# Mean over the last axis: an exit in which four engines only report, and GpSimd clears early and awaits the last store

## The chip, the cores and the metric

One core of a Trainium2 chip. The metric is the device time of one execution in microseconds (us). In the ten profiles it is 1.4 to 1.9 us longer than the span, because the span runs from the first to the last instruction of the kernel, and the measured time also holds part of what the runtime does around it.

## The reference

```python
def setup_inputs():
    return {"x": np.random.randn(64, 256, 8192).astype(np.float32)}

def reference(x):
    return np.mean(x, axis=2)
```

537 MB are read, and 16,384 means are written.

## The kernel before

The rows are loaded in 8 MB pieces into three buffers by SyncE's DMA queue. VectorE sums them, ScalarE helps at the end. The last 4 MB come in shrinking chunks so that little is left to sum after the last byte, and the final 512 bytes are stored by SyncE:

```python
    untracked(scaled_sum(fin[1][:, 0:1], fin_in[:, 0 : lastw + k]))._wait_ge(sem, 16)
    with tc.issue_after(st.ins):
        last_store = store_last(1)      # transpose on VectorE, DMA issued by SyncE
```

The exit is rewritten by hand after the program is built. A barrier of two semaphores stands there: each engine *reports* by a DRAIN that adds 1 to a gather semaphore (number 96), GpSimd *gathers* (waits for 4, takes 4 off), and *releases* the others by adding 4 to a second semaphore (97), on which each of them waits and takes 1 off. In between GpSimd *clears* the kernel's own semaphores (99 to 116) for the next execution. In the kernel before, the gather also waits for the last store:

```python
    drain, gather, release, _, clear = [
        i for i in exit_ins if i.engine == mybir.EngineType.Pool
    ][:5]
    ...
        for w in waits:
            if w.id != stored:
                nc.sync.wait_ge(bass.SemaphoreHandle(w.ant_name, w.id), w.wait_value)
    bass.BassInstruction(gather)._wait_ge(
        bass.SemaphoreHandle(last_store.ins.sync_info.on_update[0].ant_name, stored), 16
    )
    ...
    end_bb.instructions = [
        *awaits.instructions, *exit_ins[1 : exit_ins.index(drain)], drain, gather, clear, release
    ]
```

Of the kernel before, what the change touches and what calls it, by code (L numbers as in the profile page):

```python
# [18 lines left out]
def kernel(  # L19
# [5 lines left out]
    nc = tc.nc  # L25
# [26 lines left out]
    load_sem = [tc.alloc_semaphore(f"load{i}") for i in range(LOAD_SEMS)]  # L52
    tail_sem = [tc.alloc_semaphore(f"tail{i}") for i in range(len(LAST_CHUNKS) + 1)]
# [42 lines left out]
    def store_last(r):  # L96
        nc.vector.transpose(out=fin_t[r][:], in_=fin[r][:])  # L97
        return nc.sync.dma_start(out=out_last[r], in_=fin_t[r][0:P:SQ, :])
# [50 lines left out]
    with tc.issue_after(st.ins):  # L149
        last_store = store_last(1)  # L150
# [20 lines left out]
    blocks = nc.main_func.blocks  # L171
    end_bb, parent = blocks[2], nc.bb_map[body_bb.name]
# [3 lines left out]
    with nc.body("scratch", parent=parent, valid_engines=[DVE]):  # L176
        over = nc.vector.br_eq(nc.vector.zero_reg, 0, end_bb.name, "skipped").ins
    made = {b.name: b for b in blocks}
# [13 lines left out]
        name=nc.get_next_instruction_name(), engine=DVE, associate_branch=over.name  # L192
# [8 lines left out]



    exit_ins = list(end_bb.instructions)
    waiter, waits = exit_ins[0], exit_ins[0].sync_info.on_wait
    assert waiter.engine == mybir.EngineType.SP and isinstance(waiter, mybir.InstDrain)
    stored = last_store.ins.sync_info.on_update[0].id
    drain, gather, release, _, clear = [
        i for i in exit_ins if i.engine == mybir.EngineType.Pool
    ][:5]  # L210
    assert isinstance(clear, mybir.InstISA)
    with nc.body("awaits", parent=parent, valid_engines=[mybir.EngineType.SP]):
        for w in waits:
            if w.id != stored:
                nc.sync.wait_ge(bass.SemaphoreHandle(w.ant_name, w.id), w.wait_value)
    bass.BassInstruction(gather)._wait_ge(
        bass.SemaphoreHandle(last_store.ins.sync_info.on_update[0].ant_name, stored), 16
    )
    awaits = next(b for b in blocks if b.name == "awaits")
    blocks.remove(awaits)  # L220
    end_bb.instructions = [
        *awaits.instructions, *exit_ins[1 : exit_ins.index(drain)], drain, gather, clear, release
    ]


# [28 lines left out]
```

## Time and profile before

| | before |
|---|---|
| time, three runs | 1246.15 us (1246.12 to 1246.19) |
| span of the profiled run | 1244.4 us |
| DMA | 431 GB/s over the span |
| time of the profiled run (not one of the three) | 1246.25 us |
| last transpose ends | 1242.49 us |
| last store: issued, landed | 1242.515, 1244.063 us |
| last instruction ends | 1244.426 us |

The stream of loads sets all but the last 4 us. The change can only act after the last store has been issued, so that is where to read: the instructions of the exit, which do not count as busy time, and the trace's records of when each semaphore was counted. Two of those semaphores matter: that of the last store (116) and that of the runtime's own barrier behind the kernel (2), which is counted nine times per round. No view of the profile prints these counts; here and below they are read from the trace's records. A DMA has *landed* when its semaphore makes its last count. In the views, PEld is TensorE, ACT ScalarE, DVE VectorE, SP SyncE and POOL GpSimd; a q behind the name marks an instruction that does not count as busy.

### The profile page before, as it was taken

Reading aid. Unit: us, or ns where it says so; the run is one execution under the profiler, and the core shown is the slowest. Engines: PE = TensorE matmul, PEld = TensorE weight load, DVE = VectorE, ACT = ScalarE, POOL = GpSimd, SP = SyncE. Lnnn points to the kernel's source line nnn. Section 1 sums busy time; section 2 is a strip of 40 time slices with the busy share of each in tenths; the row PEclk is TensorE's granted clock in tenths of the full one; section 3 lists DMA queues with packets and bytes.
Section 4 is the critical chain, followed back from the end, with each engine's and each line's share of the span. In section 5 each row is a group of like instructions: output and inputs, shape, how many; then the busy total and the mean of one; then the engine's idle time right before and its main releaser. Section 6 shows DMA issues by size and latency. Waiting matters only on the chain.

```text
span 1244.4 us, 203 instructions
## 1 busy us (share of the span) xinstructions
DVE 1087.0 (87%) x78; ACT 16.5 (1%) x13; POOL 0.2 (0%) x4
## 2 busy tenths in 40 slices
DVE  2898988989889889898898988989889898898898
ACT  0000000000000000000000000000000000000004
POOL 0000000000000000000000000000000000000000
DMA  9999999999999999999999999999999999999998
GB/s 432 423 426 438 438 438 438 436 430 415 438 438 438 438 438 432 417 432 438 438 438 438 432 417 432 438 438 438 438 436 419 426 438 438 438 438 436 426 419 373
DMA packets 10241, 536.95 MB, mean 431 GB/s; under 512 B 1280, under 2 KB 1536, under 8 KB 1792
## 3 DMA queue, kind: packets, MB, share of 16 engines
q1 hardware_dynamic: 10240, 536.94, 99.8%
q14 instruction: 1, 0.01, 0.0%
HBM read 536.87 MB, written 0.07 MB: 431 GB/s over the span
## 4 chain that ended last, share of the span: by engine, by line
DMA 70%; DVE 29%; SPq 0%; issue 0%; DVEq 0%
DMA xt<-in_x_dram 70%; DVE res L80 29%; DVE fin_in L80 0%; SPq L70 0%; DVE fin_in L86 0%; DVE fin_t L97 0%; DVEq L86 0%
## 5 line engine op out<-in xcount | busy, mean ns | idle before, releaser
L80 DVE TENSOR_REDUCE res<-xt 128x2 f32<-128x16384 f32 (+1 forms) x63 | 1076.3, 17085 | 153.1 <-DMA xt<-in_x_dram 153.1
L83 ACT ACT_TABLE_LOAD x1 | 1.3, 1283 | 1181.0 <-DVE res L80 1181.0
L83 ACT ACTIVATE xt<-xt 128x8192 f32<-128x8192 f32 (+5 forms) x6 | 14.7, 2444 | 43.9 <-DMA xt<-in_x_dram 43.7
L80 DVE TENSOR_REDUCE fin_in<-xt 128x1 f32<-128x256 f32 (+3 forms) x5 | 5.0, 1005 | 0.3 <-DMA xt<-in_x_dram 0.2
L80 DVE TENSOR_REDUCE head<-xt 128x1 f32<-128x4096 f32 x1 | 4.4, 4420 | 0.7 <-DMA xt<-in_x_dram 0.7
L83 ACT ACTIVATION_READ_ACCUMULATOR xt<-xt 128x1 f32 x6 | 1.1, 186 | 0.0
L60 DVE MEMSET fin<- 128x32 f32 x2 | 0.1, 85 | 0.9 <-PEq L238 0.9
L86 DVE TENSOR_SCALAR_CACHE_REDUCE fin_in<-fin_in 128x265 f32<-128x265 f32 x1 | 0.4, 430 | 0.2 <-DVE fin_in L80 0.2
L97 DVE STREAM_TRANSPOSE fin_t<-fin 128x32 f32<-128x32 f32 x2 | 0.4, 212 | 0.1
L138 DVE TENSOR_SCALAR bulk<-res 128x126 f32<-128x126 f32 x1 | 0.2, 228 | 0.1
L86 DVE TENSOR_SCALAR_CACHE_REDUCE head<-head 128x2 f32<-128x2 f32 x1 | 0.2, 154 | 0.1
L238 POOL MEMSET const-bfloat16-1.0<- 128x1 bf16 x1 | 0.1, 102 | 0.0
L238 POOL MEMSET const-uint8-127<- 128x1 uint8 x1 | 0.1, 102 | 0.0
L238 POOL MEMSET const-float32-0.0<- 128x1 f32 x1 | 0.1, 99 | 0.2 <-issue 0.2
L238 POOL MEMSET const-float32-1.0<- 128x1 f32 x1 | 0.1, 99 | 0.0
L86 DVE DVE_READ_ACCUMULATOR fin_in<-fin_in 128x1 f32 x1 | 0.1, 83 | 0.0
L86 DVE DVE_READ_ACCUMULATOR head<-head 128x1 f32 x1 | 0.1, 82 | 0.0
## 6 DMA issues: line engine op xcount, KB each, us to landing
xt<-in_x_dram SPq DMA_DIRECT2D x1, 4096.0 KB, 31.2
xt<-in_x_dram SPq DMA_DIRECT2D x1, 2048.0 KB, 35.7
xt<-in_x_dram SPq DMA_DIRECT2D x1, 1024.0 KB, 37.7
xt<-in_x_dram SPq DMA_DIRECT2D x63, 40.8
xt<-in_x_dram SPq DMA_DIRECT2D x1, 512.0 KB, 38.5
xt<-in_x_dram SPq DMA_DIRECT2D x1, 256.0 KB, 38.7
xt<-in_x_dram SPq DMA_DIRECT2D x1, 128.0 KB, 38.6
fin_in<-in_x_dram SPq DMA_DIRECT2D x1, 128.0 KB, 38.5
```

Source lines behind the costliest of these rows:

```text
L60: nc.vector.memset(fin[r][:], 0.0)
L80: return untracked(nc.vector.tensor_reduce(out=dst, in_=src, axis=X, op=ADD))
L83: return untracked(nc.scalar.activation(out=src, in_=src, func=COPY, accum_out=dst))
L86: return nc.vector.tensor_scalar(out=src, in0=src, scalar1=inv, scalar2=None, op0=mybir.AluOpType.mult, op1=ADD, accum_out=dst,)
L97: nc.vector.transpose(out=fin_t[r][:], in_=fin[r][:])
L138: nc.vector.tensor_scalar_mul(out=bulk[:], in0=res[:], scalar1=inv)
L238: nc = _bacc.Bacc("TRN2", target_bir_lowering=False, num_devices=1)
```

## The change

The intent: engines that have reported need not be held, so the release goes; and the clear of the semaphores can run while the last store is still in flight, if that store's semaphore is left out and taken back to zero by the wait on it.

```diff
-    with nc.body("awaits", parent=parent, valid_engines=[mybir.EngineType.SP]):
-    ... (waits of SyncE, same in both)
...
-    bass.BassInstruction(gather)._wait_ge(
-        bass.SemaphoreHandle(last_store.ins.sync_info.on_update[0].ant_name, stored), 16
-    )
...
+    last_sem = bass.SemaphoreHandle(*sems[stored][:1], stored)
+    with nc.body("clears", parent=parent, valid_engines=[POOL]):
+        nc.gpsimd.sem_clear(range(used[0], stored))
+        nc.gpsimd.wait_ge(last_sem, 16).then_inc(last_sem, -16)
+    ...
+    reports = [
+        i
+        for i in exit_ins[1 : exit_ins.index(next(i for i in exit_ins if i.engine == POOL))]
+        if isinstance(i, mybir.InstDrain)
+    ]
+    drain, gather = [i for i in exit_ins if i.engine == POOL][:2]
     end_bb.instructions = [
-        *awaits.instructions, *exit_ins[1 : exit_ins.index(drain)], drain, gather, clear, release
+        *made["awaits"].instructions, *reports, drain, gather, *made["clears"].instructions
     ]
```

(`...` marks lines left out, here and in the cuts below.)

## The prediction

> **What bounds the kernel now.** I read the page first: the chain that ended last, then the same chain in order of time, then the views of single source lines for what stands after it. On the page:
>
> ```profile
> span 1244.4 us, 203 instructions
> DVE 1087.0 (87%) x78; ACT 16.5 (1%) x13; POOL 0.2 (0%) x4
> HBM read 536.87 MB, written 0.07 MB: 431 GB/s over the span
> DMA 70%; DVE 29%; SPq 0%; issue 0%; DVEq 0%
> ```
>
> The reader sees a kernel that streams 537 MB at one steady rate: the page's row of DMA tenths is 9 in all slices but the last, so the loads set the time. The 29% given to VectorE are reductions that free a buffer for a load already queued behind others. GpSimd (POOL) works for 0.2 us in all. The change touches nothing before the last load, so only the tail matters. The chain in order of time, from the last load on:
>
> ```profile
> 1201.66 38.49 DMA xt<-in_x_dram
> ...
> 1241.80 0.45 DVE fin_in L86 x2
> 1242.27 0.21 DVE fin_t L97
> ```
>
> The chain stops at 1242.48 with the transpose of the last results, but the span is 1244.4: some 1.9 us come after the last piece of arithmetic, in the store and the exit. These do not count as busy work, and the view of the lines that issue them shows them. First the last store's issue, the later of two, and the two waits of SyncE's exit (columns: engine and operation, count, shortest/median/longest ns, first and last start in us):
>
> ```profile
> L98 SPq DMA_DIRECT2D out_dram<-fin_t x2: 522/580/637, 1236.5 to 1242.5; - x2
> L215 SPq EVENT_SEMAPHORE  x2: 28/28/28, 1243.1 to 1243.2; - x2
> ```
>
> Then the exit itself, all under one line:
>
> ```profile
> L156 POOLq EVENT_SEMAPHORE  x2: 17/262/506, 1243.6 to 1244.3; - x2
> L156 POOLq DRAIN  x1: 41/41/41, 0.8 to 0.8; - x1
> L156 PEldq DRAIN  x1: 8/8/8, 0.9 to 0.9; - x1
> L156 ACTq DRAIN  x1: 536/536/536, 1240.9 to 1240.9; - x1
> L156 DVEq DRAIN  x1: 10/10/10, 1242.5 to 1242.5; - x1
> L156 SPq DRAIN  x1: 311/311/311, 1243.2 to 1243.2; - x1
> L156 POOLq EVENT_SEMAPHORE_RANGE_CLEAR  x1: 136/136/136, 1244.2 to 1244.2; - x1
> L156 SPq EVENT_SEMAPHORE  x1: 17/17/17, 1244.4 to 1244.4; - x1
> L156 PEldq EVENT_SEMAPHORE  x1: 51/51/51, 1244.4 to 1244.4; - x1
> ```
>
> To be seen here: four engines report by a DRAIN, SyncE last; GpSimd's first semaphore instruction (the gather) is the 506 ns one; the clear comes after it, then the 17 ns release, then each engine's wait on the release. The trace's records with their starts to the nanosecond, and its records of semaphore counts, give this ledger (us): store issued 1242.515, issue ends 1243.037; SyncE's DRAIN 1243.250 to 1243.561; gather 1243.586 to 1244.092; the last store's semaphore makes a first step at 1243.454 and its last at 1244.063; clear 1244.156 to 1244.292; release 1244.321 to 1244.338; TensorE's wait on it ends 1244.426, which is the end of the span. So **the store's landing at 1244.063 sets the exit**: the gather had SyncE's report at 1243.563 and sat 0.50 us for the store.
>
> **What the Trainium skill says.** (1) "DMA: Bandwidth & Descriptors", "Why a DMA increments its semaphore by 16 and not by 1": a transfer on fewer than 16 engines jumps by 16 less that number at once, and only the full 16 means landed. The trace agrees: the store writes four rows, and its semaphore shows one early step and then four, from 1244.005 to 1244.063. (2) The same page, "Anatomy of one DMA", puts most of about 2 us fixed cost into the receipt of the write. Here issue to landing is 1244.063 - 1242.515 = 1.55 us, less than the figure; nothing in the change shortens it. (3) "Perfetto Trace Analysis", "Sequencer-only Instruction", says that the wait for semaphores is not in the profiled duration. This trace differs for an instruction with two waits: the gather's 506 ns contain the wait for its second one. (4) "Runtime: NRT & Kernel Launch", "The ~15µs preamble/postamble breakdown": behind the kernel stand a barrier passed from engine to engine on a sync semaphore (about 44 ns a hop, 8 hops), a reset of semaphores of 51 an engine, and another barrier. The trace shows it: semaphore 2 is counted nine times from 1244.661 to 1245.184, semaphores 7 to 255 are reset between 1245.080 and 1245.785, and nine more counts run from 1246.009 to 1246.366. The eight hops ahead of the kernel took 0.371 us together, 46 ns each.
>
> That last point matters, since the reported time, 1246.15, is some 1.8 us more than the span: the measure includes this tail, so **the gain counts only if the runtime's barrier starts moving sooner**.
>
> **The change, part by part.**
>
> Removed: GpSimd's release, and the other four engines' waits on it. GpSimd saves from the end of the wait for the store to the end of the release: 1244.338 - 1244.092 = 0.246 us. It consists of 64 ns to the clear, 136 ns of clear, 29 ns to the release and 17 ns of release. The other engines leave the kernel at their DRAIN, SyncE at 1243.561 instead of about 1244.38, TensorE at 0.9 us.
>
> Moved: the clear goes ahead of the wait for the store. The gather now waits for the reports alone, and starts at 1243.586 as before. With the 17 ns that the gather at the kernel's entry takes, it ends 1243.603; 64 ns on, the clear starts at 1243.667, and takes 136 ns (17 semaphores instead of 18, no difference that I would count): 1243.803. With 29 ns to the next instruction, GpSimd waits from 1243.832 on, 0.23 us before the landing at 1244.063. **The clear is hidden whole**, with that 0.23 us to spare.
>
> Added: one wait that takes 16 off. The gather already subtracts in one instruction with its waits, and ended 29 ns after the landing. The single-wait form may start some 23 ns after the count and take 17 ns, so 1244.092 to 1244.103. I take 0.01 us off the gain.
>
> So GpSimd leaves at about 1244.10 instead of 1244.338: 0.24 us. The span, which ended with TensorE's wait at 1244.426, should end with GpSimd at 1244.10: 0.33 us less.
>
> Who holds up the runtime's barrier? Its hops after the kernel are 34, 205, 44, 23, 98, 38, 34 and 47 ns; ahead of the kernel they were 35, 38, 43, 24, 112, 38, 35 and 46. Only the third count is late, by 0.167 us. To name its engine I use the resets: five blocks of about 51, in which 207 to 255 start at 1245.080, right after the middle of the chain, 156 to 206 at 1245.201, then 105 to 155 and 54 to 104, and 7 to 53 last at 1245.441. If the chain runs out and back and each engine resets after its last count, the turning point resets first, and the order out is that of the blocks from the bottom: TensorE, ScalarE, GpSimd, VectorE, SyncE. This is an inference, the trace does not name them. Then the late one is **GpSimd**, 0.553 us after its last count (1244.347), and TensorE's first count comes 0.22 us after its own exit. If GpSimd's 0.553 us are a fixed cost behind its last instruction, its count comes 0.24 us sooner, at 1244.66, and everything behind follows by the same amount, since the four others have been waiting by then. Gain 0.24 us: 1246.15 - 0.24 = **1245.91 us**, 0.02%.
>
> **Rivals.** First, *another engine is the late one*, or GpSimd's 0.553 us are counted from the clear and not from its end. For it: the trace names no engine, and TensorE's delay is 0.22 us only. Then the third count would be free to come at about 1244.10 + 0.22 + 0.04 to 0.1, some 1244.4 instead of 1244.900: a gain of 0.5 us, 1245.65. Against: no other engine's exit was later than TensorE's, which was in time for the first count. Second, *the wait for the store is only handed on*: the gain would vanish if the landing moved later or if GpSimd's single wait with its subtraction took long, 1246.1 to 1246.2. Against: the same engine subtracts in its gather with no visible cost, and the store is issued by an unchanged path. Third, *SyncE becomes the bound*: its report at 1243.563 plus the clear would have to end after the landing. There are 0.23 us of room; a store landing that much faster would leave the clear partly exposed, at worst 0.1 to 0.2 us less gain, with the landing earlier by the same. Fourth, *no effect at all*, if the measured time ended on something other than this chain; then 1246.15.
>
> **Range and chances.** I give the first account about 6 in 10, a larger gain (0.3 to 0.55 us) 2 in 10 and a smaller or no gain 2 in 10. The three runs lie within 0.07 us (1246.12 to 1246.19), so noise is smaller than the effect. Range 1245.60 to 1246.15. Two per cent are 24.9 us; the whole tail from the transpose to the last count is 1246.366 - 1242.487 = 3.9 us, so even deleting it would not reach that. Within 2%: 0.99, the rest is left for a surprise in the stream.
>
> **What would show it.** The changed trace should show a 17 to 30 ns gather at 1243.6, a clear near 1243.67 while the store is out, GpSimd's last instruction ending some 30 ns after the last count of the store, no waits on the release, a span 0.33 us shorter, and a third count of semaphore 2 about 0.55 us after GpSimd's end. If it comes 0.2 us after, the first rival holds. The prediction is wrong if the loads' stretch moves by more than 0.1 us, if the clear runs after the landing, or if the time after the span grows by what the span loses.

## The result, and the profile after

| | before | changed |
|---|---|---|
| time, six runs each | 1246.17 us (1246.12 to 1246.30) | 1246.00 us (1245.78 to 1246.58) |
| all runs | 24 runs, median 1246.19, mean 1246.23 | 16 runs, median 1245.94, mean 1245.99 |
| span of the profiled run | 1244.4 us | 1244.7 us |

The ratio of the changed kernel to the kernel before is 0.9999 (95% interval 0.9986 to 1.0012): the same within 2%. Pooling all runs of each kernel, the means differ by 0.23 us (95% interval, worked out from the runs' spread: 0.10 to 0.37) and the medians by 0.25 us. Two of the changed kernel's six runs came late, at 1246.41 and 1246.58. So the times alone show a gain, but not its size; the exit in the trace does.

The first thing that the profile shows is misleading. The span has grown:

```profile
span 1244.7 us, 199 instructions
...
DMA 70%; DVE 29%; SPq 0%; issue 0%; DVEq 0%
```

The reason is in the stream, far ahead of the exit. In order of time, where VectorE's reductions start in the changed kernel (start, duration, and in brackets the idle time before):

```profile
41.58 17.22 DVE L80 TENSOR_REDUCE res<-xt 128x2 f32<-128x16384 f32 x1 [2.11 <-DMA xt<-in_x_dram]
...
80.46 17.22 DVE L80 TENSOR_REDUCE res<-xt 128x2 f32<-128x16384 f32 x1 [2.29 <-DMA xt<-in_x_dram]
99.98 17.22 DVE L80 TENSOR_REDUCE res<-xt 128x2 f32<-128x16384 f32 x1 [2.29 <-DMA xt<-in_x_dram]
119.40 17.22 DVE L80 TENSOR_REDUCE res<-xt 128x2 f32<-128x16384 f32 x1 [2.20 <-DMA xt<-in_x_dram]
```

and the same in the kernel before:

```profile
41.40 17.22 DVE L80 TENSOR_REDUCE res<-xt 128x2 f32<-128x16384 f32 x1 [2.11 <-DMA xt<-in_x_dram]
...
80.11 17.22 DVE L80 TENSOR_REDUCE res<-xt 128x2 f32<-128x16384 f32 x1 [2.14 <-DMA xt<-in_x_dram]
99.46 17.22 DVE L80 TENSOR_REDUCE res<-xt 128x2 f32<-128x16384 f32 x1 [2.13 <-DMA xt<-in_x_dram]
118.80 17.22 DVE L80 TENSOR_REDUCE res<-xt 128x2 f32<-128x16384 f32 x1 [2.13 <-DMA xt<-in_x_dram]
```

The lag grows from 0.18 us at 41 us to 0.60 us at 119 us and stays near that to the end (0.57 at the issue of the last store): the buffers of this execution simply arrived later in its first 120 us. In the changed kernel's trace some of the 64 KB packets of that stretch took up to 2.69 us, against 2.43 in the kernel before. Whether the change did that is a question for the experiments. To read the exit, all times must be taken from the issue of the last store, not from the start.

The exit of the changed kernel, all that is left of the old barrier under its line:

```profile
L156 POOLq DRAIN  x1: 41/41/41, 0.8 to 0.8; - x1
L156 PEldq DRAIN  x1: 8/8/8, 0.9 to 0.9; - x1
L156 ACTq DRAIN  x1: 536/536/536, 1241.5 to 1241.5; - x1
L156 DVEq DRAIN  x1: 10/10/10, 1243.1 to 1243.1; - x1
L156 SPq DRAIN  x1: 377/377/377, 1243.8 to 1243.8; - x1
L156 POOLq EVENT_SEMAPHORE  x1: 17/17/17, 1244.2 to 1244.2; - x1
```

The new clear, which has its own line:

```profile
L218 POOLq EVENT_SEMAPHORE_RANGE_CLEAR  x1: 135/135/135, 1244.3 to 1244.3; - x1
```

And the new wait with its subtraction:

```profile
L219 POOLq EVENT_SEMAPHORE  x1: 17/17/17, 1244.7 to 1244.7; - x1
```

The 506 ns gather has become a 17 ns one; no engine waits on a release; the clear precedes the last wait. In the trace's records the store was issued at 1243.080, the clear ran from 1244.299 to 1244.434, the store landed at 1244.629, GpSimd's wait ended at 1244.671. From issue to the end of the span it was 1.59 us, against 1244.426 - 1242.515 = 1.91 before. The counts of the runtime's semaphore 2 now point to the engines that the prediction had to infer: the first is at 1.121 us, 0.23 us behind TensorE's DRAIN, the second at 1242.155, 0.16 us behind the end of ScalarE's, and the third at 1245.232, 0.56 us behind GpSimd's last instruction. That the first is TensorE's, e2 shows below, by moving it; e6 shows the rest. There GpSimd leaves at 0.8 us, and the third count comes 0.04 us behind the second, at 1241.412; the fourth comes at 1242.547, 0.20 us behind VectorE's DRAIN; the fifth, at 1244.043, waits for SyncE.

### The profile page after: what moved, and what is told of

It is laid out like the page before. It is cut to its first block, busy times and chain, and to the rows that moved or that the text cites. A ratio compares the mean times of both kernels' runs of the same rounds, so it can differ in the third digit from the quotient of the medians. Undisturbed runs are those within 1.5% of the kernel's fastest.

```text
span 1244.7 us, 199 instructions
## 1 busy us (share of the span) xinstructions
DVE 1087.0 (87%) x78; ACT 16.5 (1%) x13; POOL 0.2 (0%) x4
## 4 chain that ended last, share of the span: by engine, by line
DMA 70%; DVE 29%; SPq 0%; issue 0%; DVEq 0%
DMA xt<-in_x_dram 70%; DVE res L80 29%; DVE fin_in L80 0%; SPq L70 0%; DVE fin_in L86 0%; DVE fin_t L97 0%; DVEq L86 0%
```

## The experiments

Eight kernels were run, five timed rounds each. All gave correct results. The theory, from here on **A**: the exit gains about 0.23 us, because GpSimd's third count in the runtime's barrier is what everything behind waits for, and it comes a fixed time behind GpSimd's last instruction. Rivals: **B**, the early-leaving engines, sitting in the runtime's barrier, disturb the stream (that would explain the wide spread and the late stream); **C**, it was the other engines' waits on the release that held the barrier.

One table for all of them. "Landing" is the last count of the last store's semaphore; "third" and "fifth" are counts of semaphore 2 after the kernel. "Time - issue" is the profiled run's time less the start of the last store's issue: it removes the stream. The time follows the runtime's barrier: in all ten profiles it lies 0.116 to 0.125 us under the last count of semaphore 2, counted from the span's start.

| kernel | issue of store | landing to third, us | landing to fifth, us | time - issue, us | median of its times, us |
|---|---|---|---|---|---|
| before (1246.25 when profiled) | 1242.515 | 0.837 | 0.904 | 3.74 | 1246.17 |
| changed | 1243.080 | 0.603 | 0.670 | 3.50 | 1246.00 |
| e1_again | 1242.528 | 0.602 | 0.670 | 3.50 | 1246.03 |
| e2_held | 1242.545 | 0.603 | 0.670 | 3.50 | 1245.90 |
| e3_no_release | 1242.668 | 0.757 | 0.823 | 3.65 | 1246.17 |
| e4_clear_first | 1242.445 | 0.681 | 0.747 | 3.58 | 1246.02 |
| e5_sp_last | 1242.361 | 0.273 | 0.340 | 3.16 | 1245.56 |
| e6_sp_all | 1242.327 | (before it) | 0.171 | 2.94 | 1245.39 |
| e7_sp_nodrain | 1242.439 | (before it) | 0.179 | 2.96 | 1245.40 |
| e8_again | 1242.386 | 0.602 | 0.669 | 3.49 | 1245.85 |

The kernel before, in nine runs each: 1246.19 us (1246.04 to 1246.54) beside e1 to e4, and 1246.14 us (1246.09 to 1246.62) beside e5 to e8.

### e1_again: the changed kernel, unedited

> The changed kernel unedited, to see whether its wide spread (1245.78 to 1246.58 over six runs, the kernel before 1246.12 to 1246.30) comes back. Theory A (the exit gains 0.23 us; the spread is chance in the first 120 us of the stream, where the profiled run lost 0.6 us): from the store's last count to the third count of semaphore 2 again 0.60 us against 0.84 before; the time where the stream is undisturbed 1245.9, the spread not tied to this kernel. Rival B (engines that sit in the runtime's barrier from 1 us on disturb the stream): the spread of some 0.8 us comes back here and in no kernel whose TensorE stays inside.

Measured: 1246.03 us (1245.82 to 1246.08), while the kernel *before* now spread from 1246.04 to 1246.54. The profiled run's store was issued at 1242.528, within 0.02 us of the kernel before. So the spread belongs to neither kernel, and the late stream of the first profile did not come back. The tail is the same within a nanosecond: 0.602 us, against 0.603.

### e2_held: TensorE kept inside

```diff
+    with nc.body("held", parent=parent, valid_engines=[mybir.EngineType.PE]):
+        nc.tensor.wait_ge(tail_sem[-1], 16)
...
+        *made["held"].instructions, *made["awaits"].instructions, *reports, drain, gather, *made["clears"].instructions
```

> The changed kernel, but TensorE is held in the kernel by a wait for the last load, so that it enters the runtime's barrier at some 1241.5 and not at 1.1 us. Theory A: same tail (0.60 us from the store's last count to the third count of semaphore 2), same time as e1_again within its spread. Rival B: spread back to 0.2 us and time 1245.9, while e1_again spreads.

Measured: 1245.90 us (1245.80 to 1246.11), the same tail. TensorE's first count moved from 1.1 us to 1242.119, ScalarE's came right behind it, and the counts from the third on did not change. Rival B falls as the cause of the spread: with and without TensorE in the barrier the times cover the same range, and the kernel before, which has no early leaver, spreads as far. As e1 did not bring the late stream back, e2 could not test for it; what delayed the stream in that one profile stays open. The kernel before has runs as late, 1246.54 and 1246.62.

### e3_no_release: only the release goes

```diff
-    end_bb.instructions = [
-        *awaits.instructions, *exit_ins[1 : exit_ins.index(drain)], drain, gather, clear, release
-    ]
+    reports = [i for i in exit_ins[1 : exit_ins.index(drain)] if isinstance(i, mybir.InstDrain)]
+    end_bb.instructions = [*awaits.instructions, *reports, drain, gather, clear]
```

> One part alone: the release and the four waits on it go, the gather still waits for the store, and the clear still follows it. Theory (GpSimd's exit sets the barrier, 0.553 us behind its last instruction): only the release's 0.046 us are saved: store's last count to the third count 0.79 us, time 1246.1. Rival (the other engines' waits on the release were what held the barrier): 0.67 us or less, time 1245.9 or less.

Measured: landing to third count 0.757 us, so 0.080 saved and not 0.046; 1246.17 us. The gather waits as before, and the clear is the last instruction:

```profile
L156 POOLq EVENT_SEMAPHORE  x1: 507/507/507, 1243.7 to 1243.7; - x1
L156 POOLq EVENT_SEMAPHORE_RANGE_CLEAR  x1: 136/136/136, 1244.3 to 1244.3; - x1
```

The other engines left 0.8 us sooner or more (SyncE, the last of them, 0.50 us ahead of the landing and no longer 0.32 behind it), and the barrier moved by 0.08: rival C falls. The surplus of 0.034 us is in the delay behind GpSimd: its last instruction is now the clear, which ends at 1244.445, and the count comes 0.528 us later, at 1244.973; behind a release or a wait it was 0.56 (1244.900 - 1244.338 and 1245.232 - 1244.671). The "fixed" delay depends a little on the last instruction; e5 and e7, where GpSimd also leaves after its clear, give 0.527.

### e4_clear_first: only the clear moves

```diff
-        if isinstance(i, mybir.InstDrain)          # the waits on the release stay
...
-    drain, gather = [i for i in exit_ins if i.engine == POOL][:2]
+    drain, gather, release = [i for i in exit_ins if i.engine == POOL][:3]
...
-        *made["awaits"].instructions, *reports, drain, gather, *made["clears"].instructions
+        *made["awaits"].instructions, *reports, drain, gather, *made["clears"].instructions, release
```

> The other part alone: the clear goes ahead of the wait for the store, the release and the waits on it stay. Theory: store's last count to the third count 0.65 to 0.68 us (0.60 of the changed kernel and the release's 0.046 to 0.08), time 1245.95 to 1246.0; TensorE then makes the first count 0.23 us after its wait, still ahead of GpSimd. Rival (the waits on the release hold the barrier): 0.80 us or more, no gain.

Measured: 0.681 us, so 0.156 saved; 1246.02 us. Here the waits on the release are all back, as the exit's line shows, and still two thirds of the gain are there:

```profile
L156 POOLq EVENT_SEMAPHORE  x2: 17/17/17, 1243.5 to 1244.1; - x2
...
L156 SPq EVENT_SEMAPHORE  x1: 17/17/17, 1244.1 to 1244.1; - x1
...
L156 PEldq EVENT_SEMAPHORE  x1: 51/51/51, 1244.1 to 1244.1; - x1
```

The two parts add up: 0.080 + 0.156 = 0.236, and both together gave 0.837 - 0.603 = 0.234.

### e5_sp_last: SyncE awaits the store

If GpSimd's exit costs 0.56 us behind its last instruction and TensorE's 0.23, GpSimd is the wrong engine to leave last. This kernel gives the last wait to SyncE, the fifth in the chain.

```diff
-        nc.gpsimd.wait_ge(last_sem, 16).then_inc(last_sem, -16)
+    with nc.body("last", parent=parent, valid_engines=[SP]):
+        nc.sync.wait_ge(last_sem, 16).then_inc(last_sem, -16)
...                                        # "last" goes to the end of the exit
```

> SyncE, not GpSimd, awaits the final store and takes its count off, behind its own report; GpSimd leaves after its clear. Theory (GpSimd's third count comes some 0.66 us after its clear begins, fixed; the barrier's fifth count waits for SyncE, whose delay behind its exit is small like TensorE's 0.23): third count no longer bound to the store, some 1.83 us after the store's issue against 2.15 in the changed kernel, time 0.3 us under it: 1245.7. Rival (SyncE has a delay as long as GpSimd's 0.55 us): fifth count 2.15 us after the store's issue against 2.22, gain under 0.1 us. Second rival (whoever waits last pays the same, the landing alone sets the barrier): no gain.

Measured: 1245.56 us (1245.42 to 1245.99); the third count comes 1244.175 - 1242.361 = 1.81 us behind the store's issue, and time less issue is 3.16, 0.34 less than the changed kernel. GpSimd still sets it, as the distance from its clear shows: 1244.175 - 1243.513 = 0.66 us, as expected.

### e6_sp_all: SyncE gathers, clears and waits

```diff
-    with nc.body("clears", parent=parent, valid_engines=[POOL]):
-        nc.gpsimd.sem_clear(range(used[0], stored))
-        nc.gpsimd.wait_ge(last_sem, 16).then_inc(last_sem, -16)
+    report = next(i for i in exit_ins[1:] if isinstance(i, mybir.InstDrain)).sync_info.on_update[0]
+    with nc.body("clears", parent=parent, valid_engines=[SP]):
+        gathered = bass.SemaphoreHandle(report.ant_name, report.id)
+        nc.sync.wait_ge(gathered, 4).then_inc(gathered, -4)
+        nc.sync.sem_clear(range(used[0], stored))
+        nc.sync.wait_ge(last_sem, 16).then_inc(last_sem, -16)
...                                        # GpSimd's DRAIN reports, SyncE's goes, SyncE's waits move behind the reports
```

> SyncE gathers the reports, clears and awaits the store; GpSimd reports at 1 us like TensorE and leaves. Theory: third count no longer limits; the fifth comes 0.2 us after SyncE's last instruction, some 1.8 us after the store's issue against 2.22 in the changed kernel: time 0.4 us under it, 1245.6. Rival (SyncE's delay is 0.55 us): gain under 0.1 us.

Measured: 1245.39 us (1245.27 to 1245.57), the fastest of all: 0.75 us under the kernel before on the same chip, 0.46 under the changed one (e8). The fifth count is at 1244.043, 0.14 us behind SyncE's last instruction, which ended at 1243.905. The clear on SyncE, on its own line:

```profile
L221 SPq EVENT_SEMAPHORE_RANGE_CLEAR  x1: 55/55/55, 1243.1 to 1243.1; - x1
```

and its wait for the store:

```profile
L222 SPq EVENT_SEMAPHORE  x1: 17/17/17, 1243.9 to 1243.9; - x1
```

The clear ends 0.69 us before the store lands (1243.872), and takes 55 ns, where GpSimd took 135 for the same 17 semaphores. Of the 0.56 us that time less issue falls below the changed kernel, 0.50 lie ahead of the fifth count, and 0.05 behind it: from the fifth to the ninth count it takes 0.163 us here and 0.162 in e7, but 0.217 or 0.218 in the other eight profiles.

### e7_sp_nodrain: e5 with a quicker report

```diff
...                                        # e5's edit
-        if isinstance(i, mybir.InstDrain)
+        if isinstance(i, mybir.InstDrain) and i.engine != SP
...
+    report = reports[0].sync_info.on_update[0]
+    bass.BassInstruction(made["awaits"].instructions[-1]).then_inc(
+        bass.SemaphoreHandle(report.ant_name, report.id), 1
+    )
```

> As e5_sp_last, but SyncE reports with its last wait and not with a DRAIN of 0.31 to 0.39 us, so that GpSimd's clear is over sooner. Theory: if GpSimd's third count still limits e5_sp_last, it comes 0.3 us sooner here, until SyncE's own end limits: time as e6_sp_all, 1245.6. Rival (SyncE limits e5_sp_last already): same time as e5_sp_last.

Measured: 1245.40 us (1245.28 to 1245.56), as e6. The third count moved to 1243.896, ahead of the landing at 1243.994, and the fifth to 1244.173, 0.179 behind it. So GpSimd's delay did limit e5, and with it out of the way SyncE's end does: the fifth count is 0.146 us behind it (1244.027). The rival (SyncE limits e5 already) falls.

### e8_again: the changed kernel beside e5 to e7

> The changed kernel once more, on the same chip as e5 to e7 to compare with them: store's last count to third count 0.60 us, time 1245.9 to 1246.0.

Measured: 1245.85 us (1245.71 to 1246.16), landing to third count 0.602. It is 0.29 us under the kernel before.

## Why the prediction was right

It said 1245.91 us and "within 2%"; the first six runs gave 1246.00 and all sixteen 1245.94. "Within 2%" was no test, as the prediction says itself: deleting the whole tail would not have reached it. The test is the tail. By its own steps:

- **Only the tail matters.** Right. The loads set all the rest: the last store was issued between 1242.33 and 1242.67 in nine of the ten profiles, whatever the exit.
- **The clear is hidden.** Right; it ended 1244.629 - 1244.434 = 0.195 us before the landing, where 1244.063 - 1243.803 = 0.26 was predicted (its 0.23 counts from 29 ns later, when the wait begins). The difference is SyncE's DRAIN, 377 ns here and 311 before; in other runs of the changed kernel it took 394 and 332.
- **The wait with its subtraction.** Right to 0.01 us: GpSimd's last instruction ended 0.042 us behind the landing; 0.03 to 0.04 was predicted.
- **The span 0.33 us less.** From the issue of the store it is 0.32 less (1.59 against 1.91). As the profile prints it, it is longer, through the stream of that execution. The time after the span grew by 0.09 us (1.82 to 1.91), which the prediction's own two figures imply (0.33 less span, 0.24 less time).
- **GpSimd is the late one, by a fixed 0.553 us behind its last count.** Right: 1245.232 - 1244.679 (its count of the store's semaphore) = 0.553. The order of the engines, inferred from the resets, is confirmed: in the changed kernel TensorE's and ScalarE's counts come first, alone, and e6 shows GpSimd, VectorE and SyncE behind them.
- **Gain 0.24 us, one to one into the time.** Measured 0.234 in the tail, 0.235 in time less issue (3.735 against 3.50), 0.23 in the pooled means, which alone would allow 0.10 to 0.37. The split that follows from its ledger was off: the release was worth 0.080 and not 0.046, the clear 0.156 and not 0.19 to 0.20. The two errors cancel in the whole. With the release gone and the clear last, GpSimd's delay is 0.034 us shorter (0.528 against 0.562); with the release kept behind the wait, the release starts 0.061 us behind the wait's end, where it came 0.029 behind the clear.
- **The noise.** This was mis-sized. "Noise is smaller than the effect" rested on three runs within 0.07 us; 24 runs of the same kernel spread over 0.58 us (1246.04 to 1246.62), more than twice the effect, and three of the sixteen runs of the changed kernel lie above the range. The prediction also named a stream that moves by over 0.1 us as a sign that it is wrong. The profiled stream did move, by 0.57 us, but e1 and e8, the same kernel, had it at 1242.53 and 1242.39, the kernel before at 1242.52: that sign does not tell a change apart from chance at this size.

The rivals: another engine as the late one is refuted by the counts and by e3; a delay counted from the clear, by e4, where the third count is 1244.673 - 1243.597 = 1.08 us behind the clear's start and still 0.56 behind GpSimd's last instruction; a wait handed on, by the wait's 0.04 us; SyncE as the bound did not occur, with 0.195 us to spare; no effect, by the time less issue. What the prediction did not see is that the 0.56 us behind GpSimd was the larger prize: e6 puts SyncE's 0.14 us in its place, and gains three times as much (0.75 us in the medians, 0.79 in time less issue).

A parenthesis was cut from its citation of "Runtime: NRT & Kernel Launch": the time of a hop stands there for the barrier ahead of the kernel, and the prediction put it behind. The figure of about 2 us that it quotes for a DMA is fitted, on that page, for transfers issued by GpSimd, which the last store is not.

## What to carry to other kernels

At the end of a kernel, let the last wait stand on the engine that gets from its last instruction into the runtime's barrier soonest and late in that barrier's order; here that is SyncE, 0.14 us behind its exit, and not GpSimd, 0.56 us. No other engine was tried as the last, and all runs are of one program. Clears and other housekeeping can run while the last store is in flight, if the store's own semaphore is left to the wait. When an effect is a quarter of a microsecond in 1246, measure it from the event before it in the trace (here the issue of the last store), where it repeated within 0.01 us over the three profiles of the changed kernel, and not in the total, which spreads by 0.6.

## What the Trainium skill lacked or had wrong

- "Runtime: NRT & Kernel Launch", "The ~15µs preamble/postamble breakdown", gives neither the order of the engines in the barrier behind the kernel nor each one's delay between its last instruction and its first count. The runs show TensorE first, then ScalarE, GpSimd, VectorE and SyncE; the delays are 0.23 us (TensorE), 0.16 (ScalarE), 0.53 to 0.56 (GpSimd), 0.20 (VectorE, in e6 alone) and 0.14 to 0.15 (SyncE, in e6 and e7).
- "Perfetto Trace Analysis", "Sequencer-only Instruction", leaves waits out of the profiled duration. With two waits in one instruction the profile counted the wait for the second: the gather of the kernel before shows 506 ns (507 in e3), the same instruction with one wait 17 ns.
- "DMA: Bandwidth & Descriptors", "Anatomy of one DMA", puts the fixed cost at about 2.0 us, from a fit for transfers issued by GpSimd; it gives none for one issued by SyncE. The last store, four rows of 128 bytes issued by SyncE, took 1.54 to 1.56 us from issue to landing in all ten profiles.
- No page has the cost of clearing a range of semaphores by one instruction: 17 of them took 135 ns on GpSimd and 55 ns on SyncE.
